# Places of no token in a mixture-of-experts kernel: an index beyond the rows, left out by gathers and sums

## The chip, the cores and the metric

The kernel runs on one core of a Trainium2 chip. The metric is the device time of one execution in microseconds (us); the number for a kernel is the median of its runs. The core's engines are TensorE (PE, with its weight loads as PEld), VectorE (DVE), ScalarE (ACT), GpSimd (POOL) and SyncE (SP). Each executes its own queue of instructions in order and waits on semaphores. Weights and plain tiles are loaded by DMAs that SP issues on a hardware queue, results and side tables leave on ScalarE's, and every transfer that goes by a list of row indices is issued by GpSimd on a software queue. All of them run on the same 16 DMA engines.

## What is computed

One decoder layer on 2048 tokens of 1024 channels in float32: a Conformer convolution module with a residual, then a mixture of experts with a residual, then a final RMSNorm. Each token picks one of 4 groups, and in it 2 of 8 experts, so there are 32 experts and 4096 assigned tokens. The part of the reference that matters here:

```python
top_val, top_idx = lax.top_k(in_grp, MOE_TOP_K)
gate = grp_p[:, None] * jax.nn.softmax(top_val, axis=-1)
expert = grp[:, None] * MOE_EXPERTS_PER_GROUP + top_idx
...
slot_tok = jnp.full((n_slots,), T, jnp.int32).at[dest].set(t_s)
slot_gate = jnp.zeros((n_slots,), jnp.float32).at[dest].set(g_s)
...
x_pad = jnp.concatenate([xt, jnp.zeros((1, D), xt.dtype)], axis=0)
xs = x_pad[slot_tok].reshape(n_blk, MOE_BLOCK, D)
...
hid = jax.nn.silu(xb @ w_gate[e]) * (xb @ w_up[e])
return hid @ w_down[e]
...
out = jnp.zeros((T + 1, D), jnp.float32).at[slot_tok].add(
    ys.astype(jnp.float32) * slot_gate[:, None])[:T]
x = x + g2 * out
return rmsnorm(x, final_g)
```

## The kernel before

**Stages.** The first stage (to about 700 us) is the convolution module: the tokens go through in four chunks of 512, the last one finished in two pieces of 256. As a piece is finished, its rows go to DRAM twice: the residual stream to `x2acc` (2048 rows and 128 more, which are set to zero once) and the normalised rows to `x1n_d`. In the second stage each expert's tokens are gathered from `x1n_d`, taken through gate, up and down products, and added to their rows of `x2acc`. At the end the rows of `x2acc` are read, normalised and written out.

**The table.** Routing gives every token a place in its two experts' segments of a table in DRAM, `tab_d`. An entry has three numbers: the row to gather, the row to add to, and the gate. The table is first filled with entries for "no token" from the tile `ini` (lines 237 to 239, written at line 823): gather row 0, add to row 2048 + p (p is the partition, so that no two places of a block share a row), gate 0. Routing then scatters the tokens' entries over it (line 678).

**Places.** The experts are sorted by their number of tokens, the first one apart, and the sorted list meets a fixed list of sizes, `PROFILE` (line 48): entry p has so many blocks of 128 places and a rest of 32 or 64. Its places add up to 4736. Below, "expert 25" is the one that meets entry 25. Filled places are at the front of an expert's blocks, in order. A block of 128 takes 128 rows of 1024 channels, one to a partition, and its weights and rows are split into two parts each for precision. A rest of 64 (or 32) is worked as 128 partitions of half (or a quarter of) a row; `small_rows` (line 737) multiplies both indices by m = 2 (or 4) and adds the part's number. Experts that overflow their places would be worked in a loop at the end (`further_blocks`, line 1185); no instruction of its body is in the trace.

**A step.** `ORDER` (line 64) lists the steps, one block or rest each: `gather` (line 1038) loads the table's entries and `fetch` (line 1050) issues the indirect gather into one of four buffers of the ring `xg`; `x_tr` transposes on TensorE; `gate_up`, `act`, `hid_tr` and `down` follow, and `down` (line 1132) issues the indirect sum into `x2acc` (line 1145). Sums of one expert wait for all sums of the expert before it. The expert at entry `LATE` = 1 has no sum: its rows are normalised and written directly by `norm` (line 1156). The first expert begins early: while the last chunk is still in the first stage, `first_rows` (line 705) gathers its first 288 places from the rows of the first three chunks into buffers of their own (`xge`, lines 724 to 730).

**Order of the work.** A planner lays out each engine's queue before the run by simulating the program with its own costs; `urgent(...)` and `high_priority(...)` shift an instruction's rank in it. On GpSimd the gathers, sums, table scatters and small arithmetic share one queue, so an instruction there that waits holds up what stands behind it. A pool with `reuse_waits` makes the first instruction that writes a buffer wait for the last use of what lay there before.

Of the kernel before, what the change touches and what calls it, by code (L numbers as in the profile page):

```python
# [14 lines left out]
U32 = mybir.dt.uint32  # L15
AF = mybir.ActivationFunctionType
OP = mybir.AluOpType
# [5 lines left out]
T = 2048  # L23
# [16 lines left out]
T0 = [sum(N[:c]) for c in range(NCH)]  # L40
# [15 lines left out]
NRB = T // P  # L56
# [71 lines left out]
def moe_kernel(ctx, tc, x, xT, cols, ada, fing, w_in, w_out, b_r, wgu, wd, out):  # L128
    nc = tc.nc
    V, S, Q = nc.vector, nc.scalar, nc.gpsimd  # L130
# [105 lines left out]
    Q.iota(ent[:].rearrange("p i q c -> p i (q c)"), pattern=[[P, NT], [0, 6]], base=0, channel_multiplier=1)  # L236
    ini = c0.tile([P, NRB, 3], I32, name="ini")
    V.memset(ini[:].bitcast(F32), 0.0)
    Q.iota(ini[:, :, 1], pattern=[[0, NRB]], base=T, channel_multiplier=1)
    ebase = c2.tile([P, E], F32, name="ebase")  # L240
    V.tensor_scalar(ebase[:], iota_row[:, :E], float(P * NRB), None, op0=OP.mult)
    euler = c2.tile([P, 4 * (G + 1)], F32, name="euler")
# [1 line left out]
    def urgent(offset=URGENT):  # L244
        return tc.high_priority(offset=offset)
# [4 lines left out]
    def bank(tag, name):  # L250
        return ps[tag].tile([P, 512], F32, tag=tag, name=name)
# [453 lines left out]
    def first_rows():  # L705

        with urgent():
            pc = bank("acc", "pcs")
            nc.tensor.matmul(pc[:, :E], ones_bf[:], Cpre[:], start=True, stop=True)
            k = sm.tile([P, 2, E], F32, tag="fk", name="fk", bufs=1)  # L710
            V.tensor_tensor(k[:, 0], oh0[:], pc[:, :E], op=OP.mult)
            V.tensor_reduce(e0[:, 0:1], k[:, 0], axis=AX.X, op=OP.add)

            d = sm.tile([P, 1 + EARLY], F32, tag="fd", name="fd", bufs=1)
            for b in range((NEARLY + P - 1) // P):
                V.tensor_scalar(d[:, 1:2], pcol[:], e0[:, 0:1], float(b * P), op0=OP.add, op1=OP.add)
                V.tensor_scalar(d[:, 1:2], d[:, 1:2], float(NEARLY), None, op0=OP.is_lt)
                V.scalar_tensor_tensor(Cpre[:], oh0[:], d[:, 1:2], Cpre[:], op0=OP.mult, op1=OP.add)
            e = nc.sync.value_load(E0[0:1, 0:1], min_val=0, max_val=E - 1)
            ft = ep.tile([P, EARLY, 3], I32, name="fte")  # L720
            nc.sync.dma_start(ft[:], tabv[ds(e, 1), :, 0:EARLY, :].rearrange("e o b c -> (e o) b c"))
            rt = ep.tile([P, 3], I32, name="rte")
            small_rows(rt, e, EARLY, EREST)
            for b in range(-1, EARLY):
                m = P // EREST if b < 0 else 1
                t = rt if b < 0 else ft[:, b, :]
                xg = ep.tile([P, D // m], F32, name=f"xge{b + 1}")
                Q.indirect_dma_start(out=xg[:], out_offset=None, in_=x1n_d[:T0[-1], :].rearrange("t (m n) -> (t m) n", m=m),
                                     in_offset=bass.IndirectOffsetOnAxis(ap=t[:, 0:1].bitcast(U32), axis=0))
                early[b] = (t, xg)  # L730
            return e

# [4 lines left out]
    def small_rows(rt, e, b, rest):  # L737

        m = P // rest
        for g in range(m):  # L740
            nc.sync.dma_start(rt[g * rest:(g + 1) * rest, :], tabv[ds(e, 1), 0:rest, b, :].rearrange("e o c -> (e o) c"))
        V.tensor_scalar(rt[:, 0:2], rt[:, 0:2], float(m), pgrp[m][:], op0=OP.mult, op1=OP.add)
# [46 lines left out]
    us, ys, zs, outs, ends = {}, {}, {}, {}, []  # L789
# [73 lines left out]
    for m in g2t:  # L863
        w, n = P // m, D // m
        for q in range(m):
            nc.sync.dma_start(g2t[m][q * w:(q + 1) * w, :], g2_d[0:1, q * n:(q + 1) * n].to_broadcast([w, n]))
    first = first_rows()
    for piece in PIECES[NCH - 1:]:
        begin(piece)
# [95 lines left out]
    xg = Ring(pool, "xg", 4, p3)  # L965
# [8 lines left out]
    ps_d = p3.enter_context(tc.tile_pool(name="ps_d", bufs=2, space=PSUM, reuse_waits="tile"))  # L974

    es, tix = {0: first}, {}
    loads, scattered, added = [], [], []

    def after_sums(d, n):

        for o in added[n][1] if len(added) >= -n else []:
            tc.add_manual_dep(d, o.name, sync, reason="the sums as they were")
# [44 lines left out]
    class Step:  # L1027
# [21 lines left out]

        def fetch(s):  # L1050
            s.xg = xg.tile([P, D], F32, name="xg")
            Q.indirect_dma_start(out=s.xg[:, :s.n], out_offset=None, in_=x1n_d[:].rearrange("t (m n) -> (t m) n", m=s.m),
                                 in_offset=bass.IndirectOffsetOnAxis(ap=s.gi, axis=0))

        def x_tr(s):
            m, nk = s.m, KD // s.m
# [75 lines left out]
        def down(s):  # L1132
            ys = xp.tile([P, D], F32, tag="ys", name="ys")
            n = min(512, s.n)
            outs = [ps_d.tile([P, 512], F32, tag="d", name="pd") for _ in range(2 if s.m == 1 else 1)]
            parts = (s.hh, s.hlo) if s.split else (s.hh,)
            for k in range(KF):
                s.products(outs, parts, ws[s.p][s.split][4 + k // 2], k, KF, k == 0, k == KF - 1)
            with tc.high_priority(offset=MOE_URGENT):
                for i, ps in enumerate(outs):  # L1140
                    sl = slice(i * n, (i + 1) * n)
                    V.tensor_tensor(ys[:, sl], ps[:, :n], g2t[s.m][:, sl], op=OP.mult)  # L1142
            s.ys = ys
            if s.p != LATE:
                d = Q.indirect_dma_start(out=x2acc[:].rearrange("t (m n) -> (t m) n", m=s.m),  # L1145
                                         out_offset=bass.IndirectOffsetOnAxis(ap=s.si, axis=0),
                                         in_=ys[:, :s.n], in_offset=None, compute_op=OP.add).ins
                if not added or added[-1][0] != s.p:
                    added.append((s.p, []))

                for o in added[-1][1]:
                    tc.declare_no_dep(d, o.name, reason="other rows")
                after_sums(d, -2)
                added[-1][1].append(d)
# [81 lines left out]
    for n in range(len(steps) + 1):  # L1236
        s = steps[n] if n < len(steps) else None
        t = steps[n - 1] if n > 0 else None
# [94 lines left out]
```

## Time and profile before

| | us |
|---|---|
| median of 3 runs | 1603.58 (1602.56 to 1604.21) |
| the profiled execution | 1605.59 |
| its span, first to last instruction | 1603.8 |
| TensorE busy | 1462.0 (91%) |
| VectorE busy | 1116.2 (70%) |
| ScalarE busy | 973.3 (61%) |
| GpSimd busy | 734.3 (46%) |
| mean granted TensorE clock | 0.964 of full speed |

Busy times are those of one profiled execution, the union of an engine's instructions; an engine that waits or issues a DMA from its sequencer is not busy. A share of the span is a mean over stages with different limits. In the chain of waits, the profile follows back from the last instruction to whatever released each step; a piece named DMA lasts from the transfer's issue to its landing. A time in brackets with an arrow, as in [7.01 <-DMA xg<-x1n_d,rt], is how long the engine had been idle before the instruction and what ended the wait. Names ending in `,ft` are of blocks of 128 places, those in `,rt` of rests.

### The profile page before, as it was taken

To read this page: it belongs to the slowest core of one execution; us is meant where nothing else is said; L and a number is where in the kernel's file an instruction comes from. 1 tells how busy PE (TensorE), PEld (TensorE's weight loads), DVE (VectorE), ACT (ScalarE), POOL (GpSimd) and SP (SyncE) were. 2 spreads that over 40 slices of the span, in tenths; PEclk is the share of its full clock that TensorE was granted. 3 is DMA by queue.
4 is the path that set the end of the run, shared out by engine and by line. 5 is a ranking of instruction groups with operands and counts; after the bars stand their busy time and mean duration, and the time that the engine had idled before them with its cause. 6 is when DMAs were issued, how large, how long until landed. Compare 5 with 4: busy or idle time off the path is not lost.

```text
span 1603.8 us, 24057 instructions
## 1 busy us (share of the span) xinstructions
PE 1462.0 (91%) x8269; PEld 1064.6 (66%) x8269; DVE 1116.2 (70%) x1779; ACT 973.3 (61%) x1600; POOL 734.3 (46%) x564
## 2 busy tenths in 40 slices
PE   5979999799999999969788799999999999999984
PEld 4856677577777776748654466555778676876763
DVE  2549988788998999874452357344569787998465
ACT  4676778877868796444420445334477667876553
POOL 0368799787689978832421212122122222222322
PEclk8999999899999999989988999999999999999987
DMA  9699898767794666682648999989899889997987
GB/s 350 242 326 324 251 305 277 238 208 263 252 339 164 233 211 236 203 318 67 230 164 235 401 324 354 346 303 366 281 384 335 273 311 355 359 351 268 363 283 278
DMA packets 123647, 455.99 MB, mean 284 GB/s; under 512 B 25594, under 2 KB 29058, under 8 KB 98946
## 3 DMA queue, kind: packets, MB, share of 16 engines
q1 hardware_dynamic: 93842, 362.48, 62.9%
q0 software_dynamic: 14224, 40.43, 9.8%
q10 hardware_dynamic: 15456, 51.51, 8.2%
q8 instruction: 66, 1.08, 0.3%
q14 instruction: 59, 0.48, 0.1%
HBM read 374.24 MB, written 80.13 MB: 283 GB/s over the span
## 4 chain that ended last, share of the span: by engine, by line
PE 62%; DMA 16%; DVE 10%; ACT 5%; issue 4%; POOL 2%; SPq 1%; ACTq 0%; POOLq 0%; DVEq 0%
PE pg L1100 15%; PE pd L1100 8%; PE pg L1102 6%; DVE acc L486 4%; PE po L384 3%; PE po L386 3%; PE po L385 3%; PE pg L384 3%; PE pa L386 2%; PE pa L384 2%; PE pa L385 2%; PE pg L386 2%; PE pg L385 2%; DMA xg<-x1n_d,rt 2%; PE pd L1102 2%
## 5 line engine op out<-in xcount | busy, mean ns | idle before, releaser
L480 POOL TENSOR_TENSOR acc<-acc,prod 128x512 f32<-128x512 f32 x321 | 430.0, 1340 | 57.0 <-ACT prod L474 35.6
L486 DVE SCALAR_TENSOR_TENSOR acc<-u,colt,acc 128x512 f32<-128x512 f32 x497 | 369.8, 751 | 20.8 <-PE acc L457 11.8
L1024 DVE TENSOR_TENSOR wl<-wraw,wh 128x1024 fp32r<-128x1024 f32 x260 | 308.3, 1230 | 65.1 <-ACT wh L1023 59.6
L474 ACT ACTIVATE prod<-u,colt 128x512 f32<-128x512 f32 x385 | 269.2, 721 | 106.9 <-POOL acc L480 77.8
L1023 ACT ACTIVATE wh<-wraw 128x1024 fp32r<-128x1024 f32 x264 | 263.9, 1057 | 97.3 <-PE pd L1100 35.9
L1100 PE MATMUL pg<-wh,xh 128*128 128x512 f32 x464 | 152.6, 400 | 10.8 <-issue 7.7
L1100 PE MATMUL pg<-wh,xl 128*128 128x512 f32 x464 | 149.4, 396 | 0.0
L1100 PE MATMUL pg<-wl,xh 128*128 128x512 f32 x464 | 148.4, 394 | 0.1
L1145 POOL DMA_INDIRECT x2acc<-ys,ft x24 | 59.3, 2470 | 175.3 <-DVE ys L1142 174.2
L1102 PE MATMUL pg<-wraw,xh 128*32 128x256 f32 (+1 forms) x992 | 124.6, 465 | 7.2 <-DVE xh L1080 4.4
L384 PE MATMUL pg<-hh,wh 128*128 128x512 f32 x256 | 105.7, 413 | 23.1 <-ACT u L416 10.8
L1145 POOL DMA_INDIRECT x2acc<-ys,rt x20 | 35.4, 1772 | 187.1 <-DVE ys L1142 121.0
L1069 ACT ACTIVATE psx<-psx,modc,A 128x128 f32<-128x128 f32 x232 | 89.3, 437 | 35.6 <-PE psx L1064 21.0
L1100 PEld LDWEIGHTS pg<-wh,xh 128*128 128x128 f32 x464 | 87.1, 190 | 33.4 <-issue 10.1
L386 PE MATMUL pg<-hh,wl 128*128 128x512 f32 x256 | 104.0, 406 | 2.3 <-DMA wl<-wi_d 2.3
L385 PE MATMUL pg<-hl,wh 128*128 128x512 f32 x256 | 105.1, 410 | 0.7 <-DVE hl L346 0.7
L384 PE MATMUL pa<-hh,wh 128*128 128x512 f32 x256 | 101.7, 397 | 1.2 <-DVE u L421 0.7
L386 PE MATMUL pa<-hh,wl 128*128 128x512 f32 x256 | 101.5, 396 | 0.7 <-DMA wl<-wi_d 0.7
L385 PE MATMUL pa<-hl,wh 128*128 128x512 f32 x256 | 101.1, 395 | 0.0
L1118 ACT ACTIVATE sg<-pg 128x256 f32<-128x256 f32 (+1 forms) x79 | 26.5, 370 | 122.5 <-PE pg L1100 63.1
L1100 PEld LDWEIGHTS pg<-wl,xh 128*128 128x128 f32 x464 | 87.5, 189 | 20.0 <-DVE wl L1024 1.7
L1100 PEld LDWEIGHTS pg<-wh,xl 128*128 128x128 f32 x464 | 87.6, 190 | 19.0 <-DVE wl L1024 0.8
(279 smaller groups left out, 2879.1 us busy)
## 6 DMA issues: line engine op xcount, KB each, us to landing
wraw<-in_wgu SPq DMA_DIRECT2D x128, 1024.0 KB
wraw<-in_wd SPq DMA_DIRECT2D x64, 1024.0 KB
adar<-in_ada SPq DMA_DIRECT2D x44, 512.0 KB
wh<-wi_d SPq DMA_DIRECT2D x42, 512.0 KB
wl<-wi_d SPq DMA_DIRECT2D x42, 512.0 KB
wraw<-in_w_in SPq DMA_DIRECT2D x22, 512.0 KB
wh<-wo_d SPq DMA_DIRECT2D x20, 512.0 KB
wl<-wo_d SPq DMA_DIRECT2D x20, 512.0 KB
```

The source lines that it names most:

```text
L384: nc.tensor.matmul(po[:, :n], wh, xh[:, :n], start=(k == 0), stop=False)
L385: nc.tensor.matmul(po[:, :n], wh, xl[:, :n], start=False, stop=False)
L386: nc.tensor.matmul(po[:, :n], wl, xh[:, :n], start=False, stop=(k == KD - 1))
L474: S.activation(pr[:, :n], u[:, k:k + n], AF.Copy, scale=wdw[:, k:k + 1])
L480: Q.tensor_tensor(acc2[:, :n], acc2[:, :n], pr[:, :n], op=OP.add)
L486: V.scalar_tensor_tensor(acc, u[:, k:k + n], wdw[:, k:k + 1], acc, op0=OP.mult, op1=OP.add)
L1023: S.activation(h[:, o], r[:, o], AF.Copy)
L1024: (Q if len(ws) == 1 and n % 3 == 2 else V).tensor_tensor(l[:, o], r[:, o], h[:, o].bitcast(F32), op=OP.subtract)
L1069: S.activation(ps[:, q, :], ps[:, q, :], AF.Identity, bias=modc[:, 24 + k:25 + k], scale=A2[:, k:k + 1])
L1100: nc.tensor.matmul(outs[o][:], st[x], mv, start=a, stop=z)
L1102: nc.tensor.matmul(outs[0][o * w:(o + 1) * w, :n], st[x], mv, start=a, stop=z, tile_position=(0, o * w))
L1145: d = Q.indirect_dma_start(out=x2acc[:].rearrange("t (m n) -> (t m) n", m=s.m), out_offset=bass.IndirectOffsetOnAxis(ap=s.si, axis=0), in_ ...
```

## The change

The entries for "no token" get row 2048 + p as the row to gather too, where row 0 stood. The gathers of the early rows and of `fetch`, and the sums in `down`, get a limit: the last valid index of their source or destination, beyond which an index is not an error and its row is left out. `norm` has no such limit, and `x2acc` keeps its 128 rows more. Since a gather then leaves the partitions of empty places as they were, the three early buffers and each of the four buffers of the ring, at its first use, are set to zero on VectorE before.

```diff
@@ -236,7 +236,7 @@
     Q.iota(ent[:].rearrange("p i q c -> p i (q c)"), pattern=[[P, NT], [0, 6]], base=0, channel_multiplier=1)
     ini = c0.tile([P, NRB, 3], I32, name="ini")
     V.memset(ini[:].bitcast(F32), 0.0)
-    Q.iota(ini[:, :, 1], pattern=[[0, NRB]], base=T, channel_multiplier=1)
+    Q.iota(ini[:, :, 0:2], pattern=[[0, NRB], [0, 2]], base=T, channel_multiplier=1)
     ebase = c2.tile([P, E], F32, name="ebase")
     V.tensor_scalar(ebase[:], iota_row[:, :E], float(P * NRB), None, op0=OP.mult)
     euler = c2.tile([P, 4 * (G + 1)], F32, name="euler")
@@ -725,8 +725,10 @@
                 m = P // EREST if b < 0 else 1
                 t = rt if b < 0 else ft[:, b, :]
                 xg = ep.tile([P, D // m], F32, name=f"xge{b + 1}")
+                V.memset(xg[:], 0.0)
                 Q.indirect_dma_start(out=xg[:], out_offset=None, in_=x1n_d[:T0[-1], :].rearrange("t (m n) -> (t m) n", m=m),
-                                     in_offset=bass.IndirectOffsetOnAxis(ap=t[:, 0:1].bitcast(U32), axis=0))
+                                     in_offset=bass.IndirectOffsetOnAxis(ap=t[:, 0:1].bitcast(U32), axis=0),
+                                     bounds_check=T0[-1] * m - 1, oob_is_err=False)
                 early[b] = (t, xg)
             return e
 
@@ -974,6 +976,7 @@
     ps_d = p3.enter_context(tc.tile_pool(name="ps_d", bufs=2, space=PSUM, reuse_waits="tile"))
 
     es, tix = {0: first}, {}
+    fetched = []
     loads, scattered, added = [], [], []
 
     def after_sums(d, n):
@@ -1049,8 +1052,12 @@
 
         def fetch(s):
             s.xg = xg.tile([P, D], F32, name="xg")
+            if len(fetched) < len(xg.pools):
+                V.memset(s.xg[:], 0.0)
+            fetched.append(s)
             Q.indirect_dma_start(out=s.xg[:, :s.n], out_offset=None, in_=x1n_d[:].rearrange("t (m n) -> (t m) n", m=s.m),
-                                 in_offset=bass.IndirectOffsetOnAxis(ap=s.gi, axis=0))
+                                 in_offset=bass.IndirectOffsetOnAxis(ap=s.gi, axis=0),
+                                 bounds_check=T * s.m - 1, oob_is_err=False)
 
         def x_tr(s):
             m, nk = s.m, KD // s.m
@@ -1144,7 +1151,8 @@
             if s.p != LATE:
                 d = Q.indirect_dma_start(out=x2acc[:].rearrange("t (m n) -> (t m) n", m=s.m),
                                          out_offset=bass.IndirectOffsetOnAxis(ap=s.si, axis=0),
-                                         in_=ys[:, :s.n], in_offset=None, compute_op=OP.add).ins
+                                         in_=ys[:, :s.n], in_offset=None, compute_op=OP.add,
+                                         bounds_check=T * s.m - 1, oob_is_err=False).ins
                 if not added or added[-1][0] != s.p:
                     added.append((s.p, []))
 
```

## Rows read from the trace of the kernel before

**Rows 1.** The page's busy time (share of the span) and instructions of each engine
```profile
PE 1462.0 (91%) x8269; PEld 1064.6 (66%) x8269; DVE 1116.2 (70%) x1779; ACT 973.3 (61%) x1600; POOL 734.3 (46%) x564
```

**Rows 2.** Stretches: us, busy time of each engine, granted clock, DMA share, GB/s
```profile
900.00:1000.00 100.00, 94.84 (x422) 62.71 (x424) 61.78 (x74) 53.39 (x85) 22.80 (x14) 0.98 0.96 357
...
1100.00:1200.00 100.00, 92.58 (x563) 69.34 (x561) 60.63 (x75) 59.86 (x100) 21.51 (x15) 0.97 0.94 347
```

**Rows 3.** The page's DMA queues: packets, MB, share of 16 engines' span
```profile
q1 hardware_dynamic: 93842, 362.48, 62.9%
q0 software_dynamic: 14224, 40.43, 9.8%
```

**Rows 4.** The chain of waits, 800 to 960: start, length, what
```profile
861.63 7.75 DMA xg<-x1n_d,rt
...
887.17 13.96 DMA wraw<-in_wd
...
901.25 15.62 DMA wraw<-in_wgu
```

**Rows 5.** The same, 1040 to 1130
```profile
1088.49 10.55 DMA x2acc<-ys,ft
...
1099.79 0.80 POOL x2acc L1145
...
1104.23 14.75 DMA xg<-x1n_d,rt
```

**Rows 6.** The same, 1500 to 1604
```profile
1533.12 4.68 DMA x2acc<-ys,rt
```

**Rows 7.** TensorE in order of time: start, length, what [idle before <-releaser]
```profile
802.72 1.07 PE L576 MATMUL lt<-two,ls 128*128 128x36 f32 x4 [4.65 <-ACT ls L564]
808.21 5.16 PE L1102 MATMUL pg<-wraw,xh 128*32 128x256 f32 x64 [4.42 <-DVE xh L1080]
...
867.42 1.11 PE L1064 MATMUL psx<-ident,xg 128*128 128x128 f32 x4 [7.01 <-DMA xg<-x1n_d,rt]
...
920.48 1.22 PE L1100 MATMUL pd<-wh,hidh 128*128 128x512 f32 x2 [3.27 <-ACT hidh L1127]
...
1113.99 1.09 PE L1064 MATMUL psx<-ident,xg 128*128 128x128 f32 x8 [1.07 <-DMA xg<-x1n_d,ft]
...
1117.09 0.73 PE L1100 MATMUL pd<-wh,hidh 128*128 128x512 f32 x2 [1.57 <-ACT hidh L1127]
1119.12 0.66 PE L1064 MATMUL psx<-ident,xg 128*128 128x128 f32 x2 [1.30 <-DMA xg<-x1n_d,rt]
```

**Rows 8.** ScalarE in order of time
```profile
1103.11 2.01 ACT L1023 ACTIVATE wh<-wraw 128x1024 fp32r<-128x1024 f32 x2 [4.70 <-DMA wraw<-in_wgu]
```

**Rows 9.** One short stretch, columns as in Rows 2
```profile
910.00:920.00 10.00, 7.21 (x38) 3.82 (x36) 8.13 (x9) 7.66 (x12) 1.76 (x1) 1.00 1.01 420
```

**Rows 10.** VectorE's groups: xcount | busy us, mean ns | idle before us
```profile
L749 DVE MEMSET wr<- 128x512 f32 x1 | 0.5, 485 | 0.1
...
L270 DVE MEMSET ca<- 128x256 f32 x1 | 0.3, 272 | 0.9 <-PEq L1321 0.9
```

**Rows 11.** VectorE in order of time
```profile
743.52 0.48 DVE L548 SCALAR_TENSOR_TENSOR x<-po,modc,x 128x256 f32<-128x256 f32 x1 [4.80 <-PE po L386]
...
859.29 0.23 DVE L742 TENSOR_SCALAR rt<-rt,pgrp 128x2 int32<-128x2 int32 x1 [9.41 <-DMA rt<-tab_d]
```

**Rows 12.** What reads the early buffers: count, duration ns min/median/max, first to last
```profile
L1064 PE MATMUL psx<-ident,xge x18: 272/273/273, 778.1 to 818.4; 128*128 128x128 f32 x18
```

**Rows 13.** GpSimd's groups, columns as in Rows 10
```profile
L678 POOL DMA_INDIRECT tab_d<-ent,hi x32 | 32.3, 1009 | 29.2 <-DVE hi L660 13.3 <-issue 9.5 <-DVE Cpre L718 5.1
L1052 POOL DMA_INDIRECT xg<-x1n_d,ft x27 | 30.3, 1123 | 127.5 <-DMA rt<-tab_d 41.8 <-PE pd L1100 34.3 <-DMA ft<-tab_d 30.6
```

**Rows 14.** GpSimd in order of time
```profile
860.31 1.01 POOL L1052 DMA_INDIRECT xg<-x1n_d,rt  x1 [9.16 <-DVE rt L742]
...
990.97 3.00 POOL L1052 DMA_INDIRECT xg<-x1n_d,rt  x1 [3.50 <-DVE rt L742]
```

## Prediction

> **What bounds the kernel now.** I began with the page's engine totals: TensorE is busy 91% of the span, VectorE 70%, GpSimd (POOL) 46% [rows 1]. A share over the whole span hides the stage, so the stretches came next. The change acts in the expert stage, from about 740 us on, and in the two stretches of it shown TensorE is busy 95 and 93 us of 100 while the DMA engines are busy 96 and 94% [rows 2]: two resources near their limits, TensorE ahead. The DMA queues say whose traffic it is: the hardware queue that loads weights takes 62.9% of the engines' time, GpSimd's software queue, which carries every gather and sum of rows, 9.8% with 40.43 MB [rows 3]. The chain of waits shows where TensorE does not set the pace: it runs through a gather before 869 us, through two weight loads from 887 to 917, through a sum and a gather from 1088 to 1119 [rows 4, 5], and through the last sum at 1533 [rows 6]. The list of TensorE's own waits says what these cost: 7.01 us before 867.42, 3.27 before 920.48, and 1.07, 1.57 and 1.30 between 1113 and 1119 [rows 7]. So the stage has a little idle time that ends with DMA, and only that can be won back. Nothing is removed from TensorE's own work.
>
> **What the change takes from the DMA queues.** The list of expert sizes holds 4,736 places for the 4,096 assigned tokens (2048 x 2), so 640 places are empty. Today they are moved all the same: 4,736 gathered rows of 4,096 B, 4,352 summed ones (all but the 384 of the expert normalised at the end) and 3 x 2 x 128 rows of that expert's last step make 40.37 MB, and 0.05 MB of table entries bring it to 40.42, against the 40.43 of the row [rows 3]. If a skipped place moves nothing, 640 gathered and 604 summed rows go (that last expert has 36 empty places whose sum is unchanged): 5.10 MB, to 35.3 MB. That is 13% of the queue, about 20 us of its 157 us (9.8% of 1603.8), and it lies beside TensorE's work nearly everywhere. What it is worth on the path, place by place (sizes of single experts are from the reference's routing of its own inputs):
>
> (a) The gathers at 860.31 and 861.63 belong to the experts 25 and 23 of the list, with 42 and 60 tokens for 64 places: 26 of 128 rows are empty, 104 KB of 512 KB. The second one's landing is 7.75 us on the chain [rows 4], and TensorE waits 7.01 us before [rows 7]. How landing time follows bytes I take from two rows: 7.75 us for the second of two gathers (512 KB in flight), 14.75 us for the third of three (1,152 KB) [rows 4, 5]: 7.0 us for 640 KB, 10.9 ns per KB, so 104 KB are worth 1.1 us. Bounds: 0 (landing is all latency) and 7.75 x 26/128 = 1.6.
>
> (b) The three gathers before 1104.23 hold 23 empty rows of 288 (expert 4's second block 18, expert 30 five): 92 KB, 1.0 us by the same slope, bounds 0 and 14.75 x 23/288 = 1.2. TensorE's waits of 1.07, 1.57 and 1.30 us there leave room for it [rows 7]; the ScalarE wait of 4.70 us for a weight load just ahead [rows 8] says that weights are late there too, and they are not changed.
>
> (c) From 887 to 917 the chain is weight loading [rows 4], with DMA at its limit, 420 GB/s [rows 9]. In it run gathers with 14, 50 and 29 empty rows (expert 0's last block, experts 20 and 28) and sums with 2 and 22 (experts 22 and 25): 117 rows, 479 KB at 4,096 B, 1.1 us at 420 GB/s; bounds 0 and 1.4 (sums counted twice, read and written). TensorE's wait of 3.27 us at the end of it covers that.
>
> (d) The last sum, expert 31, has 27 of 32 places filled: 5/32 of its 4.68 us [rows 6] is at most 0.7, at least 0. I take 0.3, nearer to latency, as only 20 KB go.
>
> Together 3.5 us, bounds 0 and 4.9. What remains late then: the table rows that the gathers need, and the weights.
>
> [...] The landing of the gather behind 867.42 ended TensorE's 7.01 us wait [rows 7]; no row tells which part of the gather came last. [...]
>
> **What the change adds.** Seven zero fills on VectorE: three for the first expert's early buffers (two of 128x1024, one of 128x256) and four of 128x1024, one at the first use of each of the four gather buffers (experts 22, 25, 23 and expert 0's last block). A fill of 512 columns takes 485 ns, of 256 columns 272 [rows 10], so 1,024 take about 911: 5.7 us in all. Each is a new wait for its gather on GpSimd, with the later sums and gathers queued behind. But VectorE stands idle 4.80 us before 743.52 and 9.41 us before 859.29 [rows 11], where a fill fits, and the early buffers are first read at 778, long after their gathers [rows 12]. All hidden costs 0, all exposed 5.7. I take 0.5, half of one fill, since both rows say hidden but the order on VectorE is laid out by the planner. The fill of a buffer that lies over the routing stage's tiles also has to wait until these were read, and then VectorE's queue stands behind it: this is in the upper bound.
>
> A limit on each of 97 indirect DMAs (47 gathers of the experts' blocks and three of the early ones; 47 sums, the three blocks of the last expert having none). No row shows an instruction with a limit. Without one, the gathers of whole rows take 1,123 ns in the mean, the table scatter, another form of the same instruction, 1,009 [rows 13], one gather 3.00 us [rows 14]. GpSimd waits most of the stage, so only those on the chain count, seven: two gathers at 860.31 and 861.63 [rows 4, 14], the sum at 1099.8 and three gathers up to 1104.23 [rows 5], the last sum at 1533 [rows 6]. I take 0.1 us each, the size of the difference between the forms, 0.7 together; bounds -0.3 (fewer rows to describe) and 7 x 2.0 = 14 (each as slow as the 3.00 us row). The wider iota of the table's initial entries and the second column are once, early, with no one waiting: 0.
>
> **The sum.** -3.5 + 0.5 + 0.7 = -2.3 us. It is made against the profiled execution, 1605.59 us with a span of 1603.8; that lies 2.0 us above the median of the runs, 1603.58. Carried over to the median: 1601.3 us. About 0.2%, 3.2 us, is what a measurement of this kernel can tell from no change, so this is inside it. With the bounds of the gain alone, 1599.9 to 1604.8.
>
> **The rivals.**
> The limit is dear: GpSimd's instruction with a limit takes longer for each row, and the seven on the chain pass this on. For it: GpSimd builds these transfers itself, and its slow row is 3.00 us beside 1.01 [rows 14]. Against: it waits most of the time. At 1.0 us more for each it gives 1601.3 + 7 x 0.9 = 1607.6; it makes the kernel measurably slower from 0.9 us each; at 2.0 us, 1614.6.
> The order moves: instructions stand in each queue as the planner's simulation lays them out, and seven more on VectorE shift it. For it: at 802.72 and 808.21 TensorE waits 4.65 and 4.42 us for work that stands in other engines' queues [rows 7]. One such gap closed gives 1601.3 - 4.4 = 1596.9, one opened 1605.7, two 1610.1. Against: the fills are ready early, in idle time.
> [...]
> Nothing is skipped on the wire: each empty place still costs its transfer. Then only costs are left, 1603.58 + 1.2 = 1604.8. The software queue's bytes would show it.
>
> **How the numbers follow.** Forecast 34%: 1601.3, of that 13 faster by over 0.2% and 21 within. Limit dear 21%: 18 slower, 3 within. Order moved 27%: 18 faster, 7 slower, 2 within. Slowest part not relieved 10% and nothing skipped 8%, both within. So faster 0.31, same 0.44, slower 0.25. The range goes from 1595 (a gap closed and the gain near its bound) to 1609 (the limit at 1.2 us each): beyond it lie the larger reorderings and the dearest limit, about 2 in 10.
>
> **What would show it.** The software queue at 35.3 MB instead of 40.43. The chain's gather of 7.75 us near 6.6, that of 14.75 near 13.7, TensorE's wait of 7.01 us shorter by about 1. Mean gather and sum times on GpSimd up by 0.1 us. Four fills of 0.9 us at the gather's line, none with TensorE waiting behind it. Wrong would be: gathers of 2 us and more, other waits before 808 us, or landings that stand.

## The result: slower, by 14 us

The changed kernel takes 1617.24 us in the median (1611.98 to 1617.71), the kernel before 1603.07 in the same job (1600.57 to 1604.21): ratio 1.0076, 95% interval 1.0050 to 1.0103. That is past the 0.2% of the prediction on the side of slower, and above its range. The profiled execution of after took 1611.98 us, with a span of 1609.9 and a mean granted clock of 0.958 (before: 1605.59, 1603.8 and 0.964).

First the page of after: engine totals, DMA packets and the software queue, which answer to [rows 1, 3].

```profile
PE 1467.9 (91%) x8269; PEld 1069.3 (66%) x8269; DVE 1128.7 (70%) x1786; ACT 975.5 (61%) x1600; POOL 738.1 (46%) x564
...
DMA packets 123647, 450.91 MB, mean 280 GB/s; under 512 B 27240, under 2 KB 30376, under 8 KB 98946
...
q0 software_dynamic: 14224, 35.35, 8.6%
```

VectorE has seven instructions more, and the software queue moved 35.35 MB instead of 40.43: the places are left out, as the change says. The chain of waits of after (start, length, what), 1040 to 1130 and the last sum, against [rows 5, 6]:

```profile
1113.15 13.96 DMA xg<-x1n_d,rt
...
1539.74 3.87 DMA x2acc<-ys,rt
```

The gather of 14.75 us is now 13.96, the last sum 3.87 instead of 4.68: both are shorter, as forecast (how much of that is the change's own is told with the prediction's terms below), and yet the kernel is slower. The loss is found by the start of the same matmul in both traces. At 342 us the one profile of after is 6.5 us ahead of before, at 808 us (the first expert's first matmul, in [rows 7]) 0.6 behind, at 1484 us 6.3 behind. A second profile of after, taken in a later job, reads +0.8, +7.3 and +16.3. So two stretches lose: from 342 to 808 us 7.1 and 6.5 us, from 808 to 1484 us 5.7 and 9.1.

The fills of after (of the early three the first and the last), VectorE in order of time (start, length, what, idle before and its releaser), with the two steps of the expert sort that follow them:

```profile
383.56 0.27 DVE L728 MEMSET xge<- 128x256 f32 x1
...
385.07 0.91 DVE L728 MEMSET xge<- 128x1024 f32 x1 [0.16 <-DVE xge L728]
...
815.18 0.91 DVE L1056 MEMSET xg<- 128x1024 f32 x1 [1.14 <-DMA x1n_d<-xr]
830.58 0.91 DVE L1056 MEMSET xg<- 128x1024 f32 x1 [1.11 <-DMA tab_d<-ent,hi]
831.66 0.91 DVE L1056 MEMSET xg<- 128x1024 f32 x1 [0.16 <-issue]
832.49 0.15 DVE L921 TENSOR_REDUCE ce<-pw 32x2 f32<-32x64 f32 x1
833.22 0.17 DVE L924 CAST Ei<-pk 1x32 int32<-1x32 f32 x1
...
857.13 0.91 DVE L1056 MEMSET xg<- 128x1024 f32 x1 [8.58 <-DMA ov_d<-ovi]
```

Each length is as forecast, 0.91 and 0.27 us. The places aren't: three stand at 384, among the convolution's work, 360 us ahead of the idle time at 743 that was to hide them; two stand right ahead of `ce`, the reduction from which the sorted expert numbers `Ei` come. The second expert's weights can't be asked for before `Ei` is cast. Before, that chain read (VectorE, then SyncE's first weight transfer behind it):

```profile
827.39 0.20 DVE L919 TENSOR_REDUCE ce<-pw 32x2 f32<-32x64 f32 x1
828.13 0.18 DVE L922 CAST Ei<-pk 1x32 int32<-1x32 f32 x1 [0.20 <-PE pk L921]
...
829.18 0.35 SPq L1016 DMA_DIRECT2D wraw<-in_wgu  x1
```

and in after the transfer is issued here:

```profile
834.25 0.35 SPq L1019 DMA_DIRECT2D wraw<-in_wgu  x1
```

From the first expert's first matmul to the cast it is 19.9 us before (828.13 - 808.21), 24.4 in after (833.22 - 808.86), 24.3 in its second profile. TensorE's waits of after, in the two places where it falls behind:

```profile
708.33 1.90 PE L576 MATMUL lt<-two,ls 128*128 128x36 f32 x8 [7.99 <-DVE y L488]
716.61 0.69 PE L523 MATMUL tT<-ident,t 128*128 128x128 f32 x2 [5.49 <-ACT t L518]
...
832.69 0.26 PE L923 MATMUL pk<-ident,ce 32*1 32x32 f32 x2 [2.72 <-DVE ce L921]
858.38 0.80 PE L1107 MATMUL pd<-wh,hidh 128*128 128x512 f32 x1 [5.14 <-DVE ys L1149]
```

In the same place near 705 the kernel before has four shorter ones, the first and the last of them:

```profile
702.88 0.44 PE L508 MATMUL yT<-ident,y 128*128 128x128 f32 x2 [1.04 <-DVE y L488]
...
718.11 0.79 PE L384 MATMUL po<-zz,wh 128*128 128x256 f32 x2 [4.95 <-ACT zz L345]
```

So there are four suspects: the limit on the indirect transfers, the early fills, the ring's fills, and the places that the planner gives to other work when fills are there.

### The profile page after: what moved, and what is told of

The parts are those of the page before. It is cut to its first block, busy times and chain, and to the rows that moved or that the text cites. A ratio compares the mean times of both kernels' runs of the same rounds, so it can differ in the third digit from the quotient of the medians.

```text
span 1609.9 us, 24162 instructions
## 1 busy us (share of the span) xinstructions
PE 1467.9 (91%) x8269; PEld 1069.3 (66%) x8269; DVE 1128.7 (70%) x1786; ACT 975.5 (61%) x1600; POOL 738.1 (46%) x564
## 2 busy tenths in 40 slices
DMA packets 123647, 450.91 MB, mean 280 GB/s; under 512 B 27240, under 2 KB 30376, under 8 KB 98946
## 3 DMA queue, kind: packets, MB, share of 16 engines
q0 software_dynamic: 14224, 35.35, 8.6%
## 5 line engine op out<-in xcount | busy, mean ns | idle before, releaser
L1107 PEld LDWEIGHTS pg<-wl,xh 128*128 128x128 f32 x464 | 87.9, 190 | 20.3 <-DVE wl L1027 0.9
```

The lines of the kernel that those rows point to most:

```text
L1107: nc.tensor.matmul(outs[o][:], st[x], mv, start=a, stop=z)
```

## The experiments

Every kernel was timed beside the kernel before on the same chip; before's medians in the four jobs were 1605.22 (the limit alone, the early fills, the ring's fills, all fills on GpSimd), 1603.80 (the ring's fills split in two ways, the early fills late, the change again), 1605.30 (the ring's fills ahead of the reduction and behind it, the whole change late, all fills on GpSimd again) and 1604.79 us (one and two transfers more, the whole change late again). Line numbers shift by a few with each edit. Where the order of instructions is told, it is that of each engine's queue, compared place by place with before's. The stage from 808 to 1484 us is the best ruler: in four kernels whose TensorE order is before's own (limits on sums, fourth fill alone, ring's fills late, all fills on GpSimd) it has before's length within 0.5 us, with one exception, 3.5 us longer in the first of two profiles of the GpSimd kernel. The stage from 342 to 808 is 0.3 to 5.0 us longer in these same kernels, without a cause in their order. So before's one profile is the shortest of six there, and a loss read against it in that stage is too large by up to as much. Where a kernel is said to be so far behind another at some place, TensorE's matmuls are matched one by one, counted from the first expert's first matmul.

### The limit alone

Before, with the limit on the 47 sums and nothing else; all queues keep their order.

```diff
-                                         in_=ys[:, :s.n], in_offset=None, compute_op=OP.add).ins
+                                         in_=ys[:, :s.n], in_offset=None, compute_op=OP.add,
+                                         bounds_check=T * s.m - 1, oob_is_err=False).ins
```

> The kernel before with the limit on the 47 sums alone; the queues of all engines stand in the order of before. If the limit is dear for GpSimd, the sums at line 1145 take 2.5 us or more in the mean instead of 1.77 (rests) and 2.47 (blocks) and the kernel is slower by 3 us or more. If the limit is cheap and the loss comes from the zero fills, this is 0 to 2 us faster than before, and the software queue moves about 2.5 MB less.

Measured: 1603.36 us, ratio 0.9988 (0.9973 to 1.0002); software queue 37.97 MB. Mean times of the sums on GpSimd (group: count | busy, mean ns | idle before):

```profile
L1145 POOL DMA_INDIRECT x2acc<-ys,ft x24 | 59.2, 2468 | 176.3 <-DVE ys L1142 175.1 <-DVE rt L742 0.8 <-issue 0.3
L1145 POOL DMA_INDIRECT x2acc<-ys,rt x20 | 34.5, 1723 | 186.4 <-DVE ys L1142 111.9 <-DMA x2acc<-ys,ft 28.3 <-DVE sg L1119 22.5
```

Before has 2470 and 1772 ns. The limit costs the sums nothing, and the rival of the dear limit falls for them; the gathers are timed below.

### The early fills alone, the ring's fills alone

Before, with `V.memset(xg[:], 0.0)` ahead of the three early gathers, and before with the four fills of the ring:

```diff
+                V.memset(xg[:], 0.0)
                 Q.indirect_dma_start(out=xg[:], out_offset=None, ...
```

> The kernel before with the three zero fills of the early buffers alone, no index changed and no limit. In the changed kernel the planner has put them at 383 us among the convolution's taps, and the order behind them is another one (825 of 7039 places in TensorE's queue). If this new order costs the first stage its time, this is 5 to 8 us slower than before. If all of the loss comes from the fills of the ring, this is within 1 us of before (2.1 us of VectorE's time at most).

Measured: 1609.88 us, ratio 1.0028 (1.0016 to 1.0040). The planner puts the three at 385 us and lays 825 of TensorE's 7039 instructions elsewhere; TensorE waits 7.99 us at 710.82 and 5.49 at 719.11, the pattern of after; from 342 to 808 us it loses 6.5 us against before's one profile, behind that nothing (-0.5). By the medians the loss is 4.7 us.

```diff
             s.xg = xg.tile([P, D], F32, name="xg")
+            if len(fetched) < len(xg.pools):
+                V.memset(s.xg[:], 0.0)
+            fetched.append(s)
```

> The kernel before with the four zero fills of the ring on VectorE alone, no index changed and no limit. If the fills wait on VectorE's queue for the transfers that last read what lay in the buffers, and TensorE behind them, this is 6 to 10 us slower than before, lost between 808 and 930 us. If the loss comes from the early fills or from the limits, it is within 1 us of before (3.6 us of VectorE's time at most).

Measured: 1611.95 us, ratio 1.0040 (1.0025 to 1.0055). The loss lies behind 808 us: 6.9 us to 1484. Its fills stand as in after, one at 814 and two around `ce`, with `Ei` cast 23.6 us behind the first expert's first matmul. Each half of the fills costs by itself, and no limit is needed for it.

### The whole change with its fills on GpSimd

All seven fills moved to GpSimd, the early ones behind the last table scatter. TensorE, VectorE, ScalarE and SyncE keep before's order.

```diff
-                V.memset(xg[:], 0.0)
+                with tc.issue_after(table_end[0]):
+                    Q.memset(xg[:], 0.0)
...
-                V.memset(s.xg[:], 0.0)
+                Q.memset(s.xg[:], 0.0)
```

> The whole change, but all seven fills on GpSimd, those of the early buffers issued behind the table's scatter; the queues of the other four engines stand in the order of before. If the loss of the change comes from the fills on VectorE (their waits and the order they bring), this is 1 to 4 us faster than before. If it comes from the limits, it is as slow as the changed kernel, 10 us or more over before.

Measured: 1602.22 us, ratio 0.9985 (0.9967 to 1.0002). Once more:

> The whole change with all seven fills on GpSimd, and the order of TensorE, VectorE, ScalarE and SyncE as in the kernel before, once more and with more rounds, to tell a gain from none. By the gain that was forecast for the transfers left out (3.5 us less 0.7 for the limits): ratio 0.998. If the smaller transfers are worth nothing where they lie: 1.000 within 0.0015.

Measured: 1603.08 us, ratio 0.9986 (0.9969 to 1.0003). Both agree on some -0.15%, and neither interval excludes none. The whole loss of the change is gone; what is left, some 2 us of gain, is near the 2.8 us that were forecast without the fills' price (3.5 - 0.7), but no gain at all is inside both intervals. Its groups on GpSimd, in the second profile:

```profile
L1059 POOL DMA_INDIRECT xg<-x1n_d,ft x27 | 33.3, 1234 | 124.6 <-DMA rt<-tab_d 47.5 <-DMA ft<-tab_d 41.0 <-PE pd L1108 15.8
L1059 POOL DMA_INDIRECT xg<-x1n_d,rt x20 | 25.7, 1287 | 38.9 <-DVE rt L745 20.8 <-DVE ib L950 7.2 <-PE pd L1108 5.3
```

A gather with a limit takes 0.07 to 0.11 us longer here than before's 1123 and 1218 ns in the mean.

### Which of the ring's fills

The fourth fill waits longest, 8.58 us in after, with VectorE's queue behind it, and TensorE waits 5.14 us right behind: the likeliest culprit by the trace. Two kernels split the four: the fourth on VectorE with the first three on GpSimd, and the reverse.

```diff
-                V.memset(s.xg[:], 0.0)
+                (Q if len(fetched) < 3 else V).memset(s.xg[:], 0.0)
```

> The kernel before with the four fills of the ring alone, the fourth on VectorE and the first three on GpSimd; the queues stand in the order of before except for these fills. The fourth fill waits on VectorE for the DMA that stores the list of further blocks, as it does in the changed kernel (8.4 to 8.6 us of idle VectorE). If that wait holds TensorE up through the products' evictions behind it, this is 3 to 5 us slower than before. If the loss of 6.4 us with all four fills on VectorE comes from the other order that the planner gave, it is within 1 us of before.

Measured: 1601.61 us, ratio 0.9986 (0.9971 to 1.0001). From 808 to 1484 us the length is before's (0.0), though the fill waits 7.70 us:

```profile
844.08 0.91 DVE L1054 MEMSET xg<- 128x1024 f32 x1 [7.70 <-DMA ov_d<-ovi]
```

The longest wait costs nothing. That theory fell. TensorE is 5.3 us behind before near 858 us and 1.2 ahead at 868: before waits 7.01 us there for a gather [rows 7], and the delay goes into that wait.

```diff
-                V.memset(s.xg[:], 0.0)
+                (V if len(fetched) < 3 else Q).memset(s.xg[:], 0.0)
```

> The kernel before with the four fills of the ring alone, the first three on VectorE and the fourth on GpSimd; all other queues stand in the order that they have with all four fills on VectorE (299 of 7039 places of TensorE's queue differ from before). If the fourth fill's wait is what costs, this is 1 to 3 us slower than before (two waits of 1.5 to 2 us on VectorE are left). If the order costs, it is 5 to 7 us slower, as with all four on VectorE.

Measured: 1614.67 us, ratio 1.0066 (1.0044 to 1.0087), 6.0 us lost from 808 to 1484. The price is that of the first three, whose own waits are 1 to 2 us. By the medians it is 10.9 us here and 6.7 with all four on VectorE, in the same TensorE order; the two intervals overlap.

### The early fills at a later place

The three early fills stay on VectorE, but behind the last count of `Cpre` at 724 us instead of at 385.

```diff
-                V.scalar_tensor_tensor(Cpre[:], oh0[:], d[:, 1:2], Cpre[:], op0=OP.mult, op1=OP.add)
+                counted = V.scalar_tensor_tensor(Cpre[:], oh0[:], d[:, 1:2], Cpre[:], op0=OP.mult, op1=OP.add)
...
+                with tc.issue_after(counted.ins):
+                    V.memset(xg[:], 0.0)
```

> The kernel before with the three fills of the early buffers on VectorE alone, issued behind the count of the first expert's places, near 728 us, in place of 385 us; 87 of 7039 places in TensorE's queue differ from before, all behind that point, in place of 825. If the early fills cost by the order that they bring to the convolution stage, this is within 1.5 us of before. If they cost by their own time or because they write there at all, it is 4 to 5 us slower, as with the fills at 385 us.

Measured: 1606.72 us, ratio 1.0010 (0.9995 to 1.0025), against 1.0028 with the fills at 385. 87 of TensorE's places differ instead of 825. TensorE's waits near 705 are before's again, the first and the last:

```profile
700.12 0.44 PE L508 MATMUL yT<-ident,y 128*128 128x128 f32 x2 [1.04 <-DVE y L488]
...
715.35 0.79 PE L384 MATMUL po<-zz,wh 128*128 128x256 f32 x2 [4.95 <-ACT zz L345]
```

So the traces point to the place, with the order that the planner lays around it, and not to the 2.1 us of filling. The intervals of the two overlap; the waits of 7.99 and 5.49 us, there in all three profiles with the fills at 384 and neither in before nor here, carry this more than the times do.

The changed kernel, once more beside them:

> The changed kernel once more, beside the variants on the same chip. If its loss is the sum of what its parts show, 4.6 us for the early fills, 6.4 for the fills of the ring and -2 for the rows left out, it is 8 to 10 us slower than before. If the parts add to each other in the stage where they meet, it is 12 us or more.

Measured: 1617.92 us, ratio 1.0077 (1.0058 to 1.0096). That is 14.1 us, more than its two halves add up to (4.7 and 6.7); what makes them dearer together was not tried.

### The ring's fills ahead of the reduction, and behind it

The same four fills on VectorE, the first three once right behind the last product of the sort (`pw`) and so ahead of `ce`, once behind the copy of the overflow counts (`ov`), some 2 us behind the cast of `Ei`. The first:

```diff
-        V.tensor_tensor(pw[:, 0, :], PM[:], cnt[:, :E], op=OP.mult)
+        counts_placed = V.tensor_tensor(pw[:, 0, :], PM[:], cnt[:, :E], op=OP.mult)
...
+                with tc.issue_after(counts_placed.ins):
+                    V.memset(s.xg[:], 0.0)
```

> The kernel before plus the four ring fills on VectorE, and nothing else of the change; the first three are told to stand right behind the last product of the expert sort (pw) and so ahead of the reduction ce, from which the expert numbers come; the fourth stands where it stood. Theory A (three fills of 0.9 us ahead of ce delay the expert numbers, the register loads and the weight transfers behind them, in a stretch where the weight transfers end last): +4 to +9 us, ratio 1.0025 to 1.0055, and ce reads its first value 2 to 4 us later than in the kernel before. Theory B (the loss of the earlier run with ring fills came from where the planner put the first fill, at 814 us, ahead of the table's work): 0 to +2 us, since no fill stands there now.

Measured: 1616.64 us, ratio 1.0081 (1.0051 to 1.0110). The second:

```diff
-    V.tensor_copy(ov[:, 3 * NOV:], nov[:, 0:1])
+    listed = V.tensor_copy(ov[:, 3 * NOV:], nov[:, 0:1])
...
+                with tc.issue_after(listed.ins):
+                    V.memset(s.xg[:], 0.0)
```

> The same four ring fills on VectorE, but the first three are told to stand behind the copy of the overflow counts (ov), so behind ce and the cast of the expert numbers; every other instruction of TensorE, ScalarE, GpSimd and the queues stands in the order of the kernel before. Theory A: the expert numbers come as early as before, ratio 0.999 to 1.001. Theory B, or a theory by which VectorE's 3.6 us cost wherever they stand near 830 us: +3 to +7 us, ratio 1.002 to 1.0045.

Measured: 1603.81 us, ratio 0.9989 (0.9967 to 1.0011). Same fills, same engine, same lengths, some 2 us between the places, and 12.8 us between the times. The first is above the 4 to 9 us that were expected. VectorE in order of time, first ahead of the reduction, then behind it (of the three fills the first and the last):

```profile
826.36 0.91 DVE L1055 MEMSET xg<- 128x1024 f32 x1 [0.16 <-issue]
...
828.78 0.91 DVE L1055 MEMSET xg<- 128x1024 f32 x1 [0.16 <-issue]
829.62 0.15 DVE L919 TENSOR_REDUCE ce<-pw 32x2 f32<-32x64 f32 x1
830.36 0.17 DVE L922 CAST Ei<-pk 1x32 int32<-1x32 f32 x1
```

```profile
825.67 0.20 DVE L919 TENSOR_REDUCE ce<-pw 32x2 f32<-32x64 f32 x1
826.41 0.18 DVE L922 CAST Ei<-pk 1x32 int32<-1x32 f32 x1 [0.20 <-PE pk L921]
828.19 0.91 DVE L1055 MEMSET xg<- 128x1024 f32 x1 [0.22 <-issue]
...
830.34 0.91 DVE L1055 MEMSET xg<- 128x1024 f32 x1 [0.16 <-issue]
```

The cast is 3.95 us earlier in the second, 3.0 when each is counted from its own first expert's first matmul (23.3 and 20.3 us). The chain of the same two kernels, in the same sequence, shows what hangs on it; before ends its weights at 901.25 + 15.62 = 916.87 [rows 4]:

```profile
891.73 15.21 DMA wraw<-in_wd
907.05 15.65 DMA wraw<-in_wgu
```

```profile
883.79 14.36 DMA wraw<-in_wd
898.27 15.61 DMA wraw<-in_wgu
```

The weights end at 922.70 with the fills ahead and at 913.88 behind. Against before, whose two profiles stand at -1.2 and -2.1 us at 808, that is 7.0 us late and 0.9 early. Stretches of TensorE at the start of it (busy, instructions, granted clock, DMA share, GB/s), before and then with the fills ahead:

```profile
824.00:832.00 8.00, 7.12 (x34) 1.00 0.23 67
832.00:840.00 8.00, 8.00 (x39) 1.00 1.00 406
```

```profile
824.00:832.00 8.00, 4.47 (x18) 0.74 0.01 2
832.00:840.00 8.00, 8.00 (x31) 0.84 0.97 363
```

The DMA engines, at a share of 0.97 from 832 to 840, stand idle until then (0.01), and TensorE loses work (18 instructions in 4.47 us against 34 in 7.12) and clock (0.74 against 1.00). From 808 to 1484 us the first kernel loses 15.2 us, the second 0.1.

### Is it the delay of the weights?

The fills ahead of `ce` delay the weights and also change the planner's order. Two kernels delay the weights without any fill: before, with one or two transfers of 1 MB, from the weights to a spare place in memory, ahead of the second expert's first weight transfer. The first differs from before in 457 of TensorE's places, the two from each other in 3.

```diff
+                e = number(steps[new].p)
+                for q in range(1):
+                    with tc.high_priority(offset=3 * URGENT):
+                        loads.append(nc.sync.dma_start(spare[q], wgu[ds(e, 1), :, 2048 * q:2048 * (q + 1)].rearrange(...)))
                 load_expert(steps[new].p, range(FIRSTL))
```

> The kernel before, with one transfer of 1 MB more on SyncE's queue, from the weights to a spare place in memory, behind the register load of the second expert's number and ahead of that expert's first weight transfer: no fill, no limit, VectorE's work unchanged, but the weight transfers start later by the time of one (some 2.5 us at the 400 GB/s that the stretch 900 to 920 shows), and the planner lays 457 of TensorE's 7039 instructions in other places. Theory D (the delay of the weights is what costs): +2.5 to +4 us, ratio 1.0015 to 1.0025. Theory O (the order that the planner lays when the weights come later is what costs): +6 to +14 us, ratio 1.004 to 1.009, as in the runs with fills ahead of the sort's reduction.

Measured: 1611.23 us, ratio 1.0040 (1.0020 to 1.0059); 3.1 us from 808 to 1484.

> The same with two such transfers; its order differs from that of the kernel with one in 3 of TensorE's 7039 places, so the two differ by the delay alone. Theory D: 2.5 to 5 us above the kernel with one transfer, ratio to the kernel before 1.003 to 1.006. Theory O: within 1.5 us of the kernel with one transfer.

Measured: 1615.14 us, ratio 1.0068 (1.0042 to 1.0095); 6.7 us from 808 to 1484. The second megabyte, with the order all but unchanged, costs 3.6 us in the profile (6.7 - 3.1) and 3.9 by the medians, as was expected of a delay; but each kernel has one profile, and the intervals of the two overlap. What the first costs with its order is not settled by the times: the profile's 3.1 us is in the range expected of the delay, the medians' 6.4 in that of the order. The places tell more. The same four transposes of TensorE (`psh`) in before, with one transfer and with two:

```profile
946.11 0.66 PE L1125 MATMUL psh<-ident,sg 128*128 128x128 f32 x4
```

```profile
946.13 0.66 PE L1126 MATMUL psh<-ident,sg 128*128 128x128 f32 x4
```

```profile
941.77 0.66 PE L1126 MATMUL psh<-ident,sg 128*128 128x128 f32 x4
```

From the first expert's first matmul (808.21, 810.60 and 802.05) that is 137.9, 135.5 and 139.7 us. The second transfer's price stands here already, 4.2 us, behind the weights that bound this stretch. With one transfer TensorE is not behind here at all, so its 3.1 us is lost later, under another order. ScalarE's conversion of weights (`wh`) at 925.13, 926.89 and 922.52 says the same, 116.9, 116.3 and 120.5 us. So delayed weights cost by themselves, as far as one profile each can show, and the loss with one transfer points to the order.

Delay doesn't give all of it, though. By the cast of `Ei` the delay is 3.4 us with the three fills ahead of `ce`, 3.7 with the ring's fills as the planner puts them and 4.5 in after; the losses from 808 to 1484 us are 15.2, 6.9 and 5.7 to 9.1. They don't follow the delay. The order's part in these no run separates. That of TensorE's lower clock two kernels show that have the same TensorE order and the same wait for `ce`, the ring's fills with all four on VectorE and with the first three:

```profile
829.15 0.26 PE L921 MATMUL pk<-ident,ce 32*1 32x32 f32 x2 [2.07 <-DVE ce L919]
```

```profile
836.59 0.21 PE L921 MATMUL pk<-ident,ce 32*1 32x32 f32 x2 [2.08 <-DVE ce L919]
```

Around it the granted clock is 0.74 from 824 to 832 us and 0.83 from 832 to 840 in the first, and 1.00 from 832 to 848 in the second. The first is 2.9 us behind the second 30 us after the first expert's first matmul (0.4 of it from ahead of the wait), 1.2 behind 71 us after it and 0.9 at 1484 us: most of what the clock costs at once is made up again within the stage, as far as one profile of each can show.

### The whole change, with its fills at the two late places

All seven fills on VectorE, the early ones behind `Cpre`'s last count, the ring's first three behind the copy of `ov`; the edits are those of the two kernels above. TensorE's, ScalarE's and SyncE's order is that of the kernel with only the early fills late.

> The whole change with all seven fills on VectorE, the three early ones told to stand behind the last count of Cpre (some 728 us), the ring's first three behind the copy of the overflow counts. If the two places cost what the change lost and nothing else did: within 0.2% of the kernel before, ratio 0.998 to 1.002, against 1.0077 of the change as it was made. If the limits, the smaller transfers or the changed start values have a cost that shows only together with the fills: above 1.004.

Measured: 1600.37 us, ratio 0.9965 (0.9944 to 0.9987). Once more:

> The whole change with its seven fills on VectorE at the two late places, once more, to settle whether it is faster than the kernel before: ratio 0.9965 to 0.998 if the first measurement and the forecast gain (2.8 us net of the fills) hold, 0.999 to 1.001 if that measurement was a lucky one.

Measured: 1601.69 us, ratio 0.9981 (0.9963 to 0.9998). Both intervals lie below 1: it is 3 to 5 us faster than the kernel before by the medians, where no more than 0.2% was expected, and 17 to 19 us better against before than the change as it was made. From 808 to 1484 us its two profiles gain 8.0 and 3.0 us, where the kernel with the same TensorE order and no transfers left out gains none (+0.1). Against that kernel they are 4.2 and 2.4 us ahead at 928 us, 6.5 and 3.4 at 1128. The chain of the first profile, against [rows 5]:

```profile
1098.63 13.88 DMA xg<-x1n_d,rt
```

## Why the prediction was wrong

**The step that failed** is the price of the fills, 0.5 us "since both rows say hidden", and with it their bound: 5.7 us if all are exposed. Their lengths were right, and with the two late places above they do hide. But the price of a fill isn't bounded by its length. It is what stands behind it: three fills ahead of `ce` hold up the expert numbers by 3.4 us, these hold up the weights, which end 7.0 us late, and the weights were what bounds the stage [rows 4, 9]. The three at 384, with the order laid around them, cost 4.7 us by the medians. The prediction had read both ends of that chain, the weight loading from 887 to 917 and the idle VectorE at 859, and had not asked which work VectorE does for the weights and where a fill may be put ahead of it.

**The rows of idle time were the wrong rows.** The idle stretches before 743.52 and 859.29 [rows 11] show that VectorE has room, not that the fill goes there. An early buffer is free long before, so the planner put its fills at 384 us; a buffer of the ring comes free near 815 us and its fill goes into the sort. The wait that the text did name, a fill over the routing stage's tiles with VectorE's queue behind it, came true with 8.58 us for the fourth fill, and costs nothing: the kernel with that fill alone on VectorE is not slower.

**The order moved** was a rival with the right mechanism and too small a price: two gaps opened, 1610.1. The early fills alone cost 4.7 us (1609.88 - 1605.22), the ring's 6.7 (1611.95 - 1605.22), the ring's put wholly ahead of the reduction 11.3 (1616.64 - 1605.30); the change loses 14.

**The limit** was taken at 0.1 us a transfer. The sums have none to show (2468 and 1723 ns with it, 2470 and 1772 without), the gathers 0.07 to 0.11. The size is right for the gathers, with luck, as it was taken from the difference of two other forms, and the dear limit is wrong.

**The gain** of 3.5 us: the queue fell to 35.35 MB, as forecast, and that nothing is skipped fell with it. Its terms hold less well. Term (a), 1.1, can be read where the order is before's, in the second profile with all fills on GpSimd (the second gather's issue, and TensorE's first instruction behind its landing), and in before:

```profile
859.90 1.04 POOL L1059 DMA_INDIRECT xg<-x1n_d,rt  x1 [0.30 <-issue]
...
867.36 1.08 PE L1072 MATMUL psx<-ident,xg 128*128 128x128 f32 x4 [0.41 <-DMA xg<-x1n_d,rt]
```

```profile
869.52 1.09 PE L1064 MATMUL psx<-ident,xg 128*128 128x128 f32 x4 [0.56 <-DMA xg<-x1n_d,rt]
```

That is 7.46 us from issue to use, 7.48 in the first such profile, and 7.89 in before (869.52 - 861.63): some 0.4 of the 1.1, so the slope of two rows was too steep. The last line also shows that the wait of 7.01 us beside which the prediction put this gather was ended by the first of the two. That first gather, with 22 of the 26 empty places by the prediction's count, comes no sooner: 6.93 and 6.96 us from issue to use, against 7.11 in before and 6.84 to 7.00 in the three kernels with the early fills alone, early or late, and with limits on the sums alone.

Term (b), 1.0 us: the gather takes 13.88 to 14.30 us in five profiles with its empty places left out, 14.63 to 14.99 in nine kernels with nothing left out. But with limits on the sums alone, so with every row gathered, it is short too:

```profile
1112.26 14.15 DMA xg<-x1n_d,rt
```

So the shorter landing can't be put down to the gather's own rows. (The 10% for "slowest part not relieved" stand for (a) and (b) both at 0. The first gather of (a) agrees; the 0.4 of the second does not, and for (b) no run decides it. Why a gather with rows left out would land no sooner, no run shows.) Term (d), 0.3, can't be seen: the last sum takes 3.75 to 4.89 us in ten kernels with nothing left out, and 3.87 to 4.86 where rows are left out. Term (c) can't be read in one row.

In sum the last kernel is 3 to 5 us faster than before, which is the forecast gain and its bound, and the 2.4 and 3.4 us of its second profile at 928 and 1128 us are near the 2.2 for (a) and (c) and the 3.2 with (b); that the first profile has 4.2 and 6.5 says how wide this is. The kernel with fills on GpSimd has some 2 us by the medians, and none in its second profile at 928 us (0.0) with the same transfers. At 1058 us it is 2.7 us behind before: both wait for `hidh` just ahead, 1.50 us against 1.43, and behind that the granted clock is 0.58 from 1044 to 1048 us and 0.57 to 1052, where before has 1.00. So the gain as a whole is shown, and its division is not.

**The forecast of no loss of TensorE's time behind a fill** ("none with TensorE waiting behind it") is what the profile contradicts most plainly: 2.72 us for `ce` and 5.14 for `ys` in after. The kernels with the first three fills and with the fourth say that the first costs and the second does not.

## What to carry to other kernels

A cheap instruction added to a half idle engine can cost what stands behind it in that engine's queue (here 11.3 us by the medians for four fills of 0.91 us, three of them ahead of `ce`), so look up which chain runs through the place where it can be put, above all a chain that ends in an address or a transfer, and pin it behind that chain. Idle time of the engine later on says nothing unless the instruction is told to stand there. Test the cost of an addition apart from its gain: here a change that was 0.8% slower held one that is 0.2 to 0.35% faster.

## What the runs showed of the hardware that was not expected

A row left out still leaves a packet. The software queue has 14224 packets before and after, while the packets under 512 B went from 25594 to 27240 and the bytes fell by 5.08 MB.

The stage from 342 to 808 us took up to 5.0 us more than in before with the very same order of instructions on every engine (the kernel with the limits on its sums alone), while the expert stage behind it repeated within 0.5 us in all such profiles but one. A profile is compared stage by stage, not by its span.

A short wait of TensorE can come with more than its length, and the same wait need not. After the wait of 2.72 us for `ce`, the changed kernel has a granted clock of 0.58 from 832 to 840 us, and 21 instructions in 7.31 us where the kernel before has 39 in 8.00 at 1.00 (shown above with the fills ahead of the reduction):

```profile
824.00:832.00 8.00, 5.08 (x24) 0.99 0.01 1
832.00:840.00 8.00, 7.31 (x21) 0.58 0.61 211
```

In its second profile the clock is 0.50 in the four microseconds from 839 us, behind the same wait. But of the two waits of 2.07 and 2.08 us that are shown above, the first came with a clock of 0.74 and 0.83 and the second left it at 1.00.
